# Halved weight loads, another product order and VectorE sums of x in a decoder layer on TensorE

## The chip, the cores and the metric

The kernel runs on one core of one Trainium2 chip. The metric is device time of one execution in microseconds (us), lower is better. Its engines are named as in the profile: PE is TensorE's matmuls and PEld its weight loads, DVE is VectorE, ACT is ScalarE, POOL is GpSimd and SP is SyncE, which here only issues DMAs. DMAs are issued by SP (hardware queue) and by POOL (software queue, which can also add what it loads to what lies in the buffer, an accumulating DMA).

## The reference

One decoder layer on a sequence of 1024 positions with 1024 channels, all in float32:

```python
h = rms_norm(x, g_mix)
z = h @ w_in + b_in                       # 1024 -> 7168 columns
va, ga, xb, gb, sa, sb = split(z)         # 1024, 1024, 1536, 1536, 1024, 1024
u = causal_conv31(va * sigmoid(ga));  u = silu(layer_norm(u));  y_a = u @ w_a_out
v = causal_conv4(xb);  v = rg_lru(v)      # gates: 16 heads of 96x96, then a linear recurrence
y_b = (v * gelu(gb)) @ w_b_out
m = sigmoid(sa) * y_a + sigmoid(sb) * y_b
x = x + m @ w_o
x = x + square(relu(rms_norm(x, g_mlp) @ w_1)) @ w_2
out = rms_norm(x, g_final)
```

A product in float32 is made of three matmuls in a faster format: each operand is split into a high part (the rounded value) and a low part (the rest), and high x high, high x low and low x high are added.

## The kernel before

Positions lie in the free dimension and channels on the partitions. The change touches the product with w_in, which is done in two parts.

**First part**, slots s = 3 to 27. Each slot makes one chunk of 128 columns of z (`chunk_mm`, L682): 48 matmuls of 128x128 by 128x512. The list `CH` gives their order: xb chunks (written XB + t, t = 0 to 11) and pairs of va and ga (VA + j, GA + j, j = 0 to 7). A slot's weight block is loaded two slots ahead by SP (`w_load`, win_raw) and split a slot ahead (`w_parts`): ScalarE writes a copy into the low part (L65) and the high part (L67), and POOL subtracts by an accumulating DMA (L66, win_l<-win_raw). That way of splitting is `split_dma`; the other, `split`, lets VectorE subtract (L414).

Behind a slot's chunk follows what hangs on the chunk before: `u_out` for a ga chunk (u, L541), or `xb_out` for an xb chunk, which writes xb and v on ScalarE (L426, L429) and queues the three further taps of v on VectorE (L438). `xb_parts`, one slot later, splits v: ScalarE writes vth (L446), VectorE the rest, vtl. `head_load` (SP, L463) gathers these into head tiles vh and vl. `head_mm(n, 0)` stands at the end of a head's slot and `head_mm(n, 1)` inside the next one (L486 to L488, 6 matmuls each); both write one and the same accumulator, which `head_gate` (ScalarE, L494) reads in between. Heads stand in slots 5 to 8, 10 to 13, 15 to 18 and 20 to 23. After each group of four, `scan_exp` and a slot later `scan_root` (ScalarE, with table loads, L510 to L518) and then `scan_tile` (VectorE, L527 to L530, 3 tiles a group) make the recurrence, whose result is stored to the scratch hd (L531).

VectorE fills the rest of its time with the taps of the width-31 convolution (`conv`, L571 to L603), 48 steps for each of 8 tiles of u; a finished tile is stored to yd (L597). `later` queues VectorE's work with the time at which it is ready, and `vector_work(end)` writes out the queue in order of those times, with convolution steps in between and then up to the planned time `end`. So the order on each engine is fixed when the kernel is built; at run time each engine works its list in order.

Most 128x1024 tiles (v, vth, vtl, g, a, u, y, xs and others) come from one pool of 37 buffers, and a new tile waits until the last reader of the tile before it in that buffer is done.

**Second part**, the columns gb, sa and sb, as 14 pairs of 128-column chunks. For each pair, a 2x2 block product (two columns by two halves of the channels, and two halves of the positions) is made with seven products instead of eight (Strassen's scheme in Winograd's form): 98 products of 12 matmuls (`z_mm`, L842). The list `zseq` holds their order as (pair, product). The sums of x that products 4 to 7 need are made at the end of the first part and the beginning of the second: `x_load`, `x_sum`, `x_parts`, placed by the table `XS` in slots 21 to 27. Before the change, `x_sum` lets ScalarE write a negated copy (L631) and POOL add the other block by an accumulating DMA from memory (L633).

A pair's weights are loaded by SP as two blocks, one for each column (`z_load`, L695, zw, 512 KB each, from a pool of four buffers), seven products ahead of the pair's first one (`z_load_to`). `z_sums` (VectorE) makes sums of weights four products ahead, `z_lhs` splits an operand three products ahead: by ScalarE (L65, L67) and an accumulating DMA (L66, zo<-zw or zo<-zs) for products 1, 2, 3, 4, 6, by ScalarE (L722) and VectorE (L414) for 5 and 7. `z_post` and `z_post2` copy an accumulator on (L878 to L889) or write an output: for gb, `z_out` takes a Gelu (ScalarE, L854), multiplies it with a half tile of the recurrence (hb, loaded from hd by `z_h`, L873, one product ahead) on VectorE (L857) and stores it to hgd (L858); for sa and sb it stores a sigmoid to the scratch gates (L865).

From the product behind the second part (yb, L91) on, nothing is changed.

Of the kernel before, what the change touches and what calls it, by code (L numbers as in the profile page):

```python
# [15 lines left out]
P = 128  # L16
# [14 lines left out]
def trunk_kernel(ctx: ExitStack, tc: tile.TileContext, x, xt_in, vecs, w_in, w_a_out, w_b_out,  # L31
# [12 lines left out]
    def T(name, dt=F32, shape=(P, S)):  # L44
        return tp.tile(list(shape), dt, tag="T", name=name)
# [17 lines left out]
    def split_dma(src, h, l):  # L63

        nc.scalar.activation(l, src, AF.Copy, scale=-1.0)  # L65
        nc.gpsimd.dma_start(l, src, accum_op=ALU.add)  # L66
        nc.scalar.activation(h, src, AF.Copy)  # L67
# [319 lines left out]
    def at(e, cost, ready=0.0):  # L387
        clk[e] = max(clk[e], ready) + cost
        return clk[e] + 0.1
# [225 lines left out]
    def x_load(c2):  # L615
        xq[c2] = q = {}
        for n in (11, 12):
            q[n] = T(f"xs{n}_{c2}")
            nc.sync.dma_start(q[n], x_blk(n, c2))

    def x_blk(n, c2):
        return xu[n % 10 - 1, 2 * (n // 10 - 1) + c2]

    def x_sum(c2, *ns):

        q = xq[c2]
        for n in ns:
            src, b = {11: (11, 12), 12: (12, 22), 22: (11, 22), 21: (22, 21)}[n]
            if n not in q:
                q[n] = T(f"xs{n}_{c2}")  # L630
            nc.scalar.activation(q[n], q[src], AF.Copy, scale=-1.0)  # L631
            at("A", 1.06)
            nc.gpsimd.dma_start(q[n], x_blk(b, c2), accum_op=ALU.add)  # L633

    def x_parts(c2, *ps):
        for p in ps:
            src = xq[c2][{6: 22, 7: 12, 5: 11, 4: 21}[p]]
            xbh[p][c2] = h = T(f"xs{p}h_{c2}", F32R)
            xbl[p][c2] = l = T(f"xs{p}l_{c2}", F32R)
            nc.scalar.activation(h, src, AF.Copy)  # L640
            later(at("A", 1.0), 1.2, nc.vector.tensor_tensor, l, src, h.bitcast(F32), ALU.subtract)
# [10 lines left out]
    def later(ready, cost, f, *a):  # L652

        todo.append((ready, len(todo), cost, f, a))
# [37 lines left out]
    def z_load(i):  # L692
        for m_ in range(2):
            zraw[i, m_] = raw = qp.tile([P, 8, P], F32, tag="p", name=f"zw{i}_{m_}", bufs=4)
            nc.sync.dma_start(raw, w_in[ZPAIRS[i] + m_])  # L695

    def z_blk(i, m_, kk):
        return zraw[i, m_][:, 4 * kk:4 * kk + 4, :]
# [34 lines left out]
    for i in range(2, NZ):  # L733
        zseq += [(i, 1), (i, 7), (i - 1, 3), (i, 6), (i, 2), (i - 1, 4), (i, 5)]
    zseq += [(NZ - 1, 3), (NZ - 1, 4)]
    def z_get(n, f):
# [8 lines left out]
    XS = {21: ((x_load, 0),), 22: ((x_sum, 0, 11, 12),), 23: ((x_sum, 0, 22), (x_load, 1)),  # L745
          24: ((x_sum, 0, 21), (x_sum, 1, 11, 12)), 25: ((x_sum, 1, 22),),
          26: ((x_parts, 0, 6, 7), (x_sum, 1, 21)), 27: ((x_parts, 0, 5, 4), (x_parts, 1, 6))}
# [3 lines left out]
    with tc.manual_schedule(engines=ENGINES):  # L751
        for s in range(3, NC1):
# [22 lines left out]
            if s == 4:  # L775
                xb_parts(0)
            elif CH[s - 2] >= XB:
                xb_parts(CH[s - 2] - XB)
# [24 lines left out]
            if s == NC1 - 3:  # L803
                z_load(0)
                z_load(1)
# [100 lines left out]
    loaded = 2  # L906

    def z_load_to(n):
        nonlocal loaded
        while loaded < min(len(zseq), n):  # L910
            if zseq[loaded][1] == 1:
                z_load(zseq[loaded][0])
            loaded += 1

    with tc.manual_schedule(engines=ENGINES):
# [40 lines left out]
        vector_work(clk["V"])  # L956
        for n in range(len(zseq) + 2):
            z_load_to(n + 7)
# [6 lines left out]
            if n + 1 < len(zseq):  # L965
                i, p = zseq[n + 1]
                if p in H_AT:
                    z_h(i, *H_AT[p])
# [61 lines left out]
    m = []  # L1030
# [678 lines left out]
```

## Time and profile before

| | |
|---|---|
| three runs | 1629.02, 1629.08, 1633.68 us, median 1629.08 |
| profiled execution | 1631.77 us, of which span 1630.0 |
| granted TensorE clock, mean | 0.993 |
| first part up to the first product of the second | 0 to 389 us of the span |
| second part | 389 to 686 us |
| the rest | 686 to 1630 us |
| PE busy, share of the span | 97% |
| DVE, ACT, POOL busy | 68%, 53%, 11% |
| DMA, hardware and software queue, share of 16 engines | 38.8% and 27.4% |

Engine rows of the profile give busy time, share and instructions. A group, a wait or a row of time names the engine, the line, the operation and out<-in by the program's tile names without their numbers. In a row of time the first number is the start in us, the second the length, and the bracket tells how long the engine had been idle before and what released it; "x3" means so many instructions in a row. A row of SPq or POOLq is that engine's DMA issue; where SP must wait to issue, its row is long. A matmul of 512 columns shows as 0.39 us but the next starts after 0.227, since matmuls overlap.

### The profile page before, as it was taken

Reading aid. Unit: us, or ns where it says so; the run is one execution under the profiler, and the core shown is the slowest. Engines: PE = TensorE matmul, PEld = TensorE weight load, DVE = VectorE, ACT = ScalarE, POOL = GpSimd, SP = SyncE. Lnnn points to the kernel's source line nnn. Section 1 sums busy time; section 2 is a strip of 40 time slices with the busy share of each in tenths; the row PEclk is TensorE's granted clock in tenths of the full one; section 3 lists DMA queues with packets and bytes.
Section 4 is the critical chain, followed back from the end, with each engine's and each line's share of the span. In section 5 each row is a group of like instructions: output and inputs, shape, how many; then the busy total and the mean of one; then the engine's idle time right before and its main releaser. Section 6 shows DMA issues by size and latency. Waiting matters only on the chain.

```text
span 1630.0 us, 18890 instructions
## 1 busy us (share of the span) xinstructions
PE 1577.1 (97%) x6910; PEld 1286.3 (79%) x6910; DVE 1115.9 (68%) x1488; ACT 858.2 (53%) x1136; POOL 176.1 (11%) x218
## 2 busy tenths in 40 slices
PE   8999999889988899899999999999999999999997
PEld 6878778767866787688888888788888888888886
DVE  6698989697777989537043136865555457888898
ACT  5538477457555665735252226654444366555552
POOL 0000000112111222101121100000000001111110
PEclk9999999999999999999999999999999999999999
DMA  9566887897787777965686442533333579888852
GB/s 368 151 172 176 217 210 199 207 266 171 206 218 193 183 186 184 298 214 143 161 208 179 117 137 83 194 123 111 103 116 118 175 233 220 224 218 211 217 129 104
DMA packets 101292, 299.14 MB, mean 184 GB/s; under 512 B 11424, under 2 KB 12960, under 8 KB 101200
## 3 DMA queue, kind: packets, MB, share of 16 engines
q1 hardware_dynamic: 70896, 208.04, 38.8%
q0 software_dynamic: 30160, 89.63, 27.4%
q8 instruction: 54, 0.88, 0.2%
q14 instruction: 38, 0.31, 0.1%
q10 hardware_dynamic: 144, 0.26, 0.0%
HBM read 146.11 MB, written 54.53 MB: 123 GB/s over the span
## 4 chain that ended last, share of the span: by engine, by line
PE 82%; issue 7%; DMA 5%; DVE 3%; ACT 1%; POOL 1%; SPq 0%; POOLq 0%; DVEq 0%; ACTq 0%
PE d L1492 14%; PE z L682 14%; PE yb L91 8%; PE ya L91 5%; PE o L1091 3%; PE e L1607 2%; DMA zo<-zw 2%; PE keep L1492 2%; PE o L91 2%; PE z L258 2%; DMA hd<-g 1%; PE rg L486 1%; PE rg L488 1%; PE rg L487 1%; DMA win_l<-win_raw 1%
## 5 line engine op out<-in xcount | busy, mean ns | idle before, releaser
L682 PE MATMUL z<-xh,win_h 128*128 128x512 f32 x400 | 125.4, 395 | 0.5 <-ACT win_h L67 0.5
L682 PE MATMUL z<-xl,win_h 128*128 128x512 f32 x400 | 124.4, 392 | 0.0
L1504 DVE TENSOR_TENSOR acc<-acc,d 128x1024 f32<-128x1024 f32 x72 | 87.9, 1220 | 33.3 <-PE d L1492 32.7
L682 PE MATMUL z<-xh,win_l 128*128 128x512 f32 x400 | 99.8, 396 | 3.4 <-DMA win_l<-win_raw 3.4
L682 PEld LDWEIGHTS z<-xh,win_l 128*128 128x128 f32 x400 | 76.2, 191 | 21.1 <-DMA win_l<-win_raw 3.9
L589 DVE SCALAR_TENSOR_TENSOR y<-u,vec,y 128x511 f32<-128x511 f32 (+14 forms) x120 | 88.5, 738 | 4.6 <-ACT y L571 4.6
L682 PEld LDWEIGHTS z<-xh,win_h 128*128 128x128 f32 x400 | 76.1, 191 | 17.9 <-ACT win_h L67 1.3
L682 PEld LDWEIGHTS z<-xl,win_h 128*128 128x128 f32 x400 | 76.2, 191 | 16.3
L494 ACT ACTIVATE g<-rg,vec 96x1024 f32<-96x1024 f32 x32 | 35.6, 1114 | 101.0 <-PE rg L488 51.6
L589 DVE SCALAR_TENSOR_TENSOR yt<-u,vec,yt 128x511 f32<-128x511 f32 (+6 forms) x112 | 82.7, 739 | 0.0
L589 DVE SCALAR_TENSOR_TENSOR y<-yt,csum,y 128x511 f32<-128x511 f32 (+6 forms) x112 | 82.7, 739 | 0.0
L438 DVE SCALAR_TENSOR_TENSOR v<-xb,vec,v 128x1023 f32<-128x1023 f32 (+2 forms) x36 | 46.2, 1283 | 20.9 <-ACT v L429 20.1
L1038 DVE TENSOR_TENSOR m<-yb,sb 128x1024 f32<-128x1024 f32 x8 | 9.8, 1225 | 71.9 <-PE yb L91 71.9
L1285 ACT ACTIVATE fa<-fa 128x512 f32<-128x512 f32 x16 | 10.1, 631 | 90.3 <-DVE fa L1263 90.3
L1225 ACT ACTIVATE o<-s 128x512 fp32r<-128x512 f32 x64 | 38.1, 622 | 29.5 <-DVE s L1217 26.1
L66 POOL DMA_DIRECT2D win_l<-win_raw x25 | 21.8, 872 | 291.7 <-ACT win_l L65 252.9
L66 POOL DMA_DIRECT2D zo<-zw x42 | 37.0, 889 | 96.9 <-ACT zo L65 71.6
L1139 DVE TENSOR_TENSOR o<-w_raw,o 128x512 fp32r<-128x512 f32 x40 | 27.5, 690 | 28.8 <-ACT o L1225 28.8
L1139 DVE TENSOR_TENSOR o<-s,o 128x512 fp32r<-128x512 f32 x64 | 42.6, 687 | 4.7 <-ACT o L1225 4.6
L1123 DVE TENSOR_TENSOR x<-xr,o 128x1024 f32<-128x1024 f32 x8 | 9.7, 1219 | 52.2 <-PE o L1091 37.7
L66 POOL DMA_DIRECT2D db_1l<-wr x7 | 6.1, 871 | 328.7 <-DMA wr<-in_w_dram 265.0
L1054 DVE TENSOR_TENSOR sa<-ya,sa 128x1024 f32<-128x1024 f32 x8 | 9.8, 1226 | 46.4 <-PE ya L91 46.4
(1582 smaller groups left out, 4638.2 us busy)
## 6 DMA issues: line engine op xcount, KB each, us to landing
fr<-fd SPq DMA_DIRECT2D x32, 512.0 KB, 5.8
wr<-in_w_dram SPq DMA_DIRECT2D x32, 512.0 KB, 6.3
w_raw<-in_w_dram SPq DMA_DIRECT2D x31, 512.0 KB, 4.4
zw<-in_w_in_dram SPq DMA_DIRECT2D x28, 512.0 KB, 4.3
win_raw<-in_w_in_dram SPq DMA_DIRECT2D x25, 512.0 KB, 6.8
win_l<-win_raw POOLq DMA_DIRECT2D x25, 512.0 KB, 6.1
zo<-zw POOLq DMA_DIRECT2D x42, 256.0 KB, 4.7
fd<-fa SPq DMA_DIRECT2D x16, 512.0 KB, 2.8
```

Source lines behind the costliest of these rows:

```text
L66: nc.gpsimd.dma_start(l, src, accum_op=ALU.add)
L91: nc.tensor.matmul(ps[:, HALVES[hf]], a, b[hf], start=i == 0, stop=i == len(todo) - 1)
L258: nc.tensor.matmul(z0[i][:, HALVES[hf]], w0[i][w][:, k, :], xpart(a, hf, k), start=k == 0 and which == "hh", stop=k == 7 and which == "hl" ...
L438: nc.vector.scalar_tensor_tensor(v[:, d:S], a[:, 0:S - d], cbw_c[:, w * 12 + t:w * 12 + t + 1], v[:, d:S], ALU.mult, ALU.add)
L494: nc.scalar.activation(a, gps.pop((n, gi))[:HD, :], AF.Sigmoid, bias=(ba_c, bx_c)[gi][:, n:n + 1])
L589: nc.vector.scalar_tensor_tensor(o[:, k:], a[:, 0:HS - k], c, o[:, k:], ALU.mult, add)
L682: nc.tensor.matmul(zps[s][:, HALVES[hf]], w[:, k, :], xw[k][part][hf], start=n == 0, stop=n == 23)
L1091: nc.tensor.matmul(ps[:, HALVES[hf]], tok(a, k, t), wo[k][b][:, HALVES[hf]], start=k == 0 and b == 0 and n == 0, stop=k == 7 and b == 1)
L1139: tt(l, src, h.bitcast(F32), ALU.subtract)
L1225: nc.scalar.activation(o[:, 0], src, AF.Copy)
L1492: nc.tensor.matmul(o, a, b, start=n == 0 and (p != 1 or g == 0), stop=n == len(todo) - 1, skip_group_check=p == 1 and g > 0)
L1504: tt(acc[p, q2], acc[p, q2], ps, ALU.add)
```

## The change

- The sums of x are made by VectorE. All four blocks of a half are loaded plainly by SP (8 loads in all, in slots 23 and 25, where before 4 were loaded in slots 21 and 23 and 8 added by POOL), and 8 subtractions on VectorE replace 8 ScalarE copies and 8 accumulating DMAs. Two of the eight splits of these sums go through `split_dma`.
- `xb_parts` follows `xb_out` in the same slot instead of in the next; the taps of v are written out ahead of it by `vector_work(0)`.
- A load of the second part's weights holds one half of the rows for both columns (two pieces of 2 KB for each partition) instead of all rows of one column (one piece of 4 KB). The first half is loaded seven products ahead of the pair's first one, the second five ahead (three for pair 2).
- In `zseq`, products 3 and 4 of the pair before change places, and the end has an order of its own.
- The loads of hb are issued three products ahead instead of one.

```diff
--- before.py
+++ after.py
@@ -613,32 +613,28 @@
     xq = {}
 
     def x_load(c2):
-        xq[c2] = q = {}
-        for n in (11, 12):
-            q[n] = T(f"xs{n}_{c2}")
-            nc.sync.dma_start(q[n], x_blk(n, c2))
-
-    def x_blk(n, c2):
-        return xu[n % 10 - 1, 2 * (n // 10 - 1) + c2]
-
-    def x_sum(c2, *ns):
-
+
+        xq[c2] = {n: T(f"xs{n}_{c2}") for n in (11, 12, 22, 21)}
+        for n, a in xq[c2].items():
+            nc.sync.dma_start(a, xu[n % 10 - 1, 2 * (n // 10 - 1) + c2])
+
+    def x_sum(c2):
         q = xq[c2]
-        for n in ns:
-            src, b = {11: (11, 12), 12: (12, 22), 22: (11, 22), 21: (22, 21)}[n]
-            if n not in q:
-                q[n] = T(f"xs{n}_{c2}")
-            nc.scalar.activation(q[n], q[src], AF.Copy, scale=-1.0)
-            at("A", 1.06)
-            nc.gpsimd.dma_start(q[n], x_blk(b, c2), accum_op=ALU.add)
+        for n, a, b in ((11, 12, 11), (12, 22, 12), (22, 22, 11), (21, 21, 22)):
+            later(0, 1.2, nc.vector.tensor_tensor, q[n], q[a], q[b], ALU.subtract)
 
     def x_parts(c2, *ps):
         for p in ps:
             src = xq[c2][{6: 22, 7: 12, 5: 11, 4: 21}[p]]
             xbh[p][c2] = h = T(f"xs{p}h_{c2}", F32R)
             xbl[p][c2] = l = T(f"xs{p}l_{c2}", F32R)
-            nc.scalar.activation(h, src, AF.Copy)
-            later(at("A", 1.0), 1.2, nc.vector.tensor_tensor, l, src, h.bitcast(F32), ALU.subtract)
+            if c2 == 0 and p < 6:
+                split_dma(src, h, l)
+                at("A", 2.0)
+            else:
+                nc.scalar.activation(h, src, AF.Copy)
+                later(at("A", 1.0), 1.2, nc.vector.tensor_tensor, l, src, h.bitcast(F32),
+                      ALU.subtract)
 
     CH = [XB, VA, GA, XB + 1, XB + 2]
     for js, g in (((1,), 1), ((2,), 2), ((3,), 3), ((4, 5, 6, 7), 4)):
@@ -689,13 +685,14 @@
     zraw, zs, zo, zb = {}, {}, {}, {}
     zn = [0]
 
-    def z_load(i):
-        for m_ in range(2):
-            zraw[i, m_] = raw = qp.tile([P, 8, P], F32, tag="p", name=f"zw{i}_{m_}", bufs=4)
-            nc.sync.dma_start(raw, w_in[ZPAIRS[i] + m_])
+    def z_load(i, kk):
+
+        zraw[i, kk] = raw = qp.tile([P, 2, 4, P], F32, tag="p", name=f"zw{i}_{kk}", bufs=4)
+        c = ZPAIRS[i]
+        nc.sync.dma_start(raw, w_in[c:c + 2, :, 4 * kk:4 * kk + 4, :].rearrange("m p k c -> p m k c"))
 
     def z_blk(i, m_, kk):
-        return zraw[i, m_][:, 4 * kk:4 * kk + 4, :]
+        return zraw[i, kk][:, m_]
 
     def z_sums(i, p):
 
@@ -731,8 +728,15 @@
     zseq = [(0, 1), (1, 1), (0, 2), (1, 2), (0, 6), (0, 7), (1, 7), (0, 5), (1, 6), (0, 3), (0, 4),
             (1, 5)]
     for i in range(2, NZ):
-        zseq += [(i, 1), (i, 7), (i - 1, 3), (i, 6), (i, 2), (i - 1, 4), (i, 5)]
-    zseq += [(NZ - 1, 3), (NZ - 1, 4)]
+        zseq += [(i, 1), (i, 7), (i - 1, 4), (i, 6), (i, 2), (i - 1, 3), (i, 5)]
+    zseq[-7:] = [(NZ - 1, p) for p in (1, 7, 6)] + [(NZ - 2, 4), (NZ - 1, 2), (NZ - 1, 5), (NZ - 2, 3)]
+    zseq += [(NZ - 1, 4), (NZ - 1, 3)]
+
+    ZL = {}
+    for i in range(2, NZ):
+        n = zseq.index((i, 1))
+        ZL[n - 7] = ((z_load, i, 0),)
+        ZL[n - (5 if i > 2 else 3)] = ((z_load, i, 1),)
     def z_get(n, f):
         return f(*zseq[n]) if 0 <= n < len(zseq) else None
 
@@ -742,9 +746,8 @@
     head_at = {s: n for n, s in enumerate(HS0)}
 
     EXP = {head_slot: g for g, head_slot in enumerate(HS0[4 * g + 3] + 1 for g in range(4))}
-    XS = {21: ((x_load, 0),), 22: ((x_sum, 0, 11, 12),), 23: ((x_sum, 0, 22), (x_load, 1)),
-          24: ((x_sum, 0, 21), (x_sum, 1, 11, 12)), 25: ((x_sum, 1, 22),),
-          26: ((x_parts, 0, 6, 7), (x_sum, 1, 21)), 27: ((x_parts, 0, 5, 4), (x_parts, 1, 6))}
+    XS = {23: ((x_load, 0),), 24: ((x_sum, 0),), 25: ((x_load, 1), (x_parts, 0, 6)),
+          26: ((x_sum, 1), (x_parts, 0, 7, 5)), 27: ((x_parts, 0, 4), (x_parts, 1, 6))}
     w_load(3)
     w_load(4)
     w_parts(3)
@@ -772,10 +775,9 @@
             elif c >= GA:
                 u_out(c - GA, zps[s - 2], zps[s - 1])
             w_parts(s + 1)
-            if s == 4:
-                xb_parts(0)
-            elif CH[s - 2] >= XB:
-                xb_parts(CH[s - 2] - XB)
+            if s == 3 or c >= XB:
+                vector_work(0)
+                xb_parts(0 if s == 3 else c - XB)
             if before is not None:
                 head_gate(before, 1, clk["P"] - 12 * MM)
             if nxt is not None:
@@ -801,8 +803,8 @@
             for f, *a in XS.get(s, ()):
                 f(*a)
             if s == NC1 - 3:
-                z_load(0)
-                z_load(1)
+                for i in range(4):
+                    z_load(i // 2, i % 2)
             vector_work(clk["P"] - 0.7)
             if nxt is not None:
                 head_load(nxt)
@@ -903,15 +905,6 @@
 
     ZX = {0: ((x_parts, 1, 7),), 7: ((later, 0, 4.8, scan_tile, 11),), 2: ((x_parts, 1, 5),), 4: ((x_parts, 1, 4),)}
     H_AT = {2: (0, 0), 5: (1, 1), 3: (0, 1), 4: (1, 0)}
-    loaded = 2
-
-    def z_load_to(n):
-        nonlocal loaded
-        while loaded < min(len(zseq), n):
-            if zseq[loaded][1] == 1:
-                z_load(zseq[loaded][0])
-            loaded += 1
-
     with tc.manual_schedule(engines=ENGINES):
 
         hg, hraw, wb0, wb0_ = [], {}, [], []
@@ -954,16 +947,18 @@
         z_get(2, z_lhs)
         u_out(7, zps[NC1 - 2], zps[NC1 - 1])
         vector_work(clk["V"])
+        z_h(0, 0, 0)
         for n in range(len(zseq) + 2):
-            z_load_to(n + 7)
+            for f, *a in ZL.get(n, ()):
+                f(*a)
             if n >= L:
                 for f, *a in ZX.get(n, ()):
                     f(*a)
             clk["A"], clk["V"] = max(clk["A"], clk["P"] + 0.5), max(clk["V"], clk["P"] - 2)
             z_get(n - 1, z_post)
             z_get(n - 2, z_post2)
-            if n + 1 < len(zseq):
-                i, p = zseq[n + 1]
+            if n + 3 < len(zseq):
+                i, p = zseq[n + 3]
                 if p in H_AT:
                     z_h(i, *H_AT[p])
             z_get(n, z_mm)
```

## The prediction

> **What bounds the kernel now.** I read the page's shares first, then the busy time by stage, then the waits of PE in the stages that the change touches, then the rows of time around the longest waits. The page:
>
> ```profile
> PE 1577.1 (97%) x6910; PEld 1286.3 (79%) x6910; DVE 1115.9 (68%) x1488; ACT 858.2 (53%) x1136; POOL 176.1 (11%) x218
> ```
>
> TensorE is the bound nearly throughout, and the change removes none of its matmuls. What it can win or lose is time in which PE waits, so I need where PE waits. Stretches of the span, PE to POOL in order, then granted clock, DMA share and GB/s:
>
> ```profile
> 50.00:280.00 230.00, 229.99 (x1008) 185.12 (x1007) 196.40 (x255) 141.95 (x147) 14.77 (x17) 1.00 0.75 192
> 280.00:389.00 109.00, 97.24 (x392) 76.43 (x392) 85.31 (x102) 65.33 (x70) 15.92 (x18) 0.92 0.89 225
> 389.00:430.00 41.00, 41.00 (x182) 33.95 (x182) 32.96 (x45) 27.21 (x45) 8.73 (x10) 1.00 0.66 173
> 430.00:540.00 110.00, 97.14 (x417) 76.95 (x416) 83.60 (x131) 57.85 (x99) 19.57 (x23) 1.00 0.75 194
> 540.00:620.00 80.00, 77.11 (x335) 62.23 (x334) 72.25 (x112) 49.49 (x86) 17.97 (x21) 1.00 0.77 191
> 620.00:686.00 66.00, 59.24 (x252) 47.17 (x251) 47.03 (x64) 44.37 (x71) 12.24 (x15) 0.99 0.89 246
> ```
>
> Two stretches show PE with hardly an idle moment and give its pace: 230.0/1008 = 0.228 us a matmul in the first part, 41.0/182 = 0.2253 in the second. At these paces the 392 matmuls of 280 to 389 need 89.4 of 109.0 us, so 19.6 us are lost there. In the second part (389 to 686) 430 to 620 holds 752 matmuls, 169.4 of 190 us, 20.6 lost; 620 to 686 holds 252, 56.8 of 66, 9.2 lost. The most that this change can win is thus about 49 us, unless it touches 686 onward, which it doesn't.
>
> **The end of the first part: removed stalls.** PE's waits, 280 to 390 (total, times, longest), and, in a second fence, rows of time around two of them:
>
> ```profile
> PE rg L486 <- ACT g L494: 4.2, 1, 4.2
> PE rg L486 <- DMA vh<-vth: 3.5, 1, 3.5
> PE z L682 <- DMA win_l<-win_raw: 3.4, 1, 3.4
> PE z L682 <- ACT win_h L67: 0.5, 1, 0.5
> ```
>
> ```profile
> 308.24 1.23 DVE L414 TENSOR_TENSOR vtl<-v,vth 128x1024 fp32r<-128x1024 f32 x1 [15.51 <-DMA hd<-g]
> ...
> 313.46 0.74 PE L486 MATMUL rg<-vh,rgh 96*96 96x512 f32 x1 [4.19 <-ACT g L494]
> ...
> 318.69 0.77 PE L682 MATMUL z<-xl,win_h 128*128 128x512 f32 x2
> ...
> 358.54 2.70 POOL L633 DMA_DIRECT2D xs<-xu  x3 [14.99 <-DVE yt L589]
> ...
> 361.23 0.92 POOL L66 DMA_DIRECT2D win_l<-win_raw  x1
> ...
> 372.80 5.52 PE L682 MATMUL z<-xh,win_l 128*128 128x512 f32 x16 [3.44 <-DMA win_l<-win_raw]
> ```
>
> The waits sum to 11.6 us; the rest of the 19.6 is the slow matmuls behind each long wait: 313.46 to 318.69 holds 12 in 5.23 us, 0.436 apiece, 2.5 us over the pace. Three times 2.5 and 11.6 are 19.1, so the account closes. The Trainium skill, TensorE: Matmul & The Clock Gate, Part 1, says that the clock halves after an idle window of some 3.4 us and returns after about as much busy time. The trace agrees in kind (4.2 us idle, then 0.436 us a matmul); by that page's 3.4 us at half pace a long stall's tail would be an estimated 1.7 us and my sum 0.8 us better.
>
> All three have one parent. The third is plain: the correction of a weight block was issued at 361.23 behind three accumulating loads of x on the same POOL queue and arrived 11.5 us later. The first begins where DVE waits 15.5 us for a store of a recurrence, whose buffer vtl takes over, while the plain loads of x occupy buffers and queues; the second is a landing in the same backlog. Transfers of 280 to 390, with KB and median us to landing:
>
> ```profile
> yd<-y SPq DMA_DIRECT2D x2, 512.0 KB, 11.3
> ...
> vh<-vth SPq DMA_DIRECT2D x1, 384.0 KB, 15.4
> ```
>
> After the change the first x loads come two slots later (slot 23) and the eight accumulating DMAs are gone, so the queue ahead of the block's correction is empty, vtl's buffer isn't taken by an x tile, and vh lands without that backlog. I take all four waits as gone: 19.6. Eight copies of 128x1024 (1.05 us by the row of 373.18 below) leave ScalarE. VectorE gets eight subtractions of 1.22 us (row of 308.24) and loses two low parts of x to an accumulating DMA on POOL (0.9 us of issue each, with POOL busy 15.9 of 109 us), 7.3 us net. It was busy for 85.3 of these 109 us, so some of its convolution taps slide into the second part. There it was busy 235.8 of 297 us, so that would fill 88% of a stretch shortened to 275. I price it at nothing; if that cover is gone, it costs up to 7.3.
>
> **Parts of v a slot sooner: an added wait.** ScalarE's high part of v now stands in the slot in which VectorE still adds three taps to v:
>
> ```profile
> 148.06 3.92 DVE L438 SCALAR_TENSOR_TENSOR v<-xb,vec,v 128x1023 f32<-128x1023 f32 x3 [0.99 <-ACT v L429]
> 149.82 1.04 ACT L446 ACTIVATE vth<-v 128x1024 fp32r<-128x1024 f32 x1
> 156.70 1.11 ACT L494 ACTIVATE g<-rg,vec 96x1024 f32<-96x1024 f32 x1
> 159.29 0.40 PE L486 MATMUL rg<-vh,rgh 96*96 96x512 f32 x1
> ```
>
> Now the copy at 149.82 is that of the chunk before. After the change ScalarE reaches there the copy of this chunk, and its v is ready at 151.98: 2.16 us of waiting, with the square roots, two table loads and the gate of 156.70 queued behind it. That gate then ends at 157.81 + 2.16 = 159.97, while the next head's first matmul, which writes the same accumulator, was due at 159.29: 0.7 us. This chain with the roots stands in slots 10, 15 and 20: 2.1 us in all. In the other slots the gate ends early enough. Bounds: nothing, if ScalarE had room elsewhere, and three times 2.2.
>
> **A new stall at the last slot.** Four x loads, then four loads of the second part's weights, now stand on SP ahead of the store of the last convolution but one. Its buffer is wanted by the next tile of taps. On VectorE a recurrence is queued behind that, and ScalarE's u waits for the recurrence's buffer; the last weight block's copies stand behind u.
>
> ```profile
> 363.06 0.69 DVE L580 TENSOR_TENSOR yt<-u 128x512 f32<-128x512 f32 x1
> ...
> 364.24 1.22 DVE L527 SCALAR_TENSOR_TENSOR g<-a,g 128x1024 f32<-128x1024 f32 x1
> ...
> 366.88 2.29 DVE L530 TENSOR_TENSOR_SCAN g<-a,g 128x1024 f32<-128x1024 f32 x1
> ...
> 369.92 1.28 ACT L541 ACT_TABLE_LOAD   x1
> ...
> 371.22 1.11 ACT L541 ACTIVATE u<-z,vec 128x1024 f32<-128x1024 f32 x1
> ...
> 373.18 1.05 ACT L67 ACTIVATE win_h<-win_raw 128x1024 fp32r<-128x1024 f32 x1
> ...
> 378.16 0.62 PE L682 MATMUL z<-xh,win_h 128*128 128x512 f32 x2
> ```
>
> Now this tile's taps end at 361.9; less the lost time ahead of it (19.6 without the last wait's 3.9 and the tail's 2.5) they would end at 348.7, and as one slot's filler goes elsewhere I take 346.5. For the store I take 8 us, less than the 11.3 of its row because the accumulating loads are gone: landed 354.5. From 363.06 to the recurrence's end at 369.17 the row takes 6.1 us, so 360.6; then 1.28, 1.11 and two copies of 1.05 make 365.1. The last slot started at 378.2 and without the 19.6 but with one 0.7 would start at 359.3. PE waits 5.8 us, with a slow tail of 2.5: 8.3. Bounds: nothing (landing 6 us sooner), and 12 (landing in the row's 11.3). First part: 19.6 − 2.1 − 8.3 = 9.2 us won.
>
> **Second part: what makes PE wait there.** PE's waits from 380 to 690 (two of sixteen lines), the landing of the hb loads there, and one pair's rows:
>
> ```profile
> PE z6e L842 <- DVE zo L414: 2.4, 1, 2.4
> ...
> PE z13f L842 <- DMA zo<-zw: 2.2, 1, 2.2
> ```
>
> ```profile
> hb<-hd SPq DMA_DIRECT2D x24, 256.0 KB, 4.9
> ```
>
> ```profile
> 489.45 6.03 SPq L858 DMA_DIRECT2D hgd<-hb  x2
> ...
> 495.20 0.61 ACT L65 ACTIVATE zo<-zw 128x512 fp32r<-128x512 f32 x1
> ...
> 495.57 5.50 SPq L695 DMA_DIRECT2D zw<-in_w_in_dram  x2
> ...
> 496.11 0.88 POOL L66 DMA_DIRECT2D zo<-zw  x1 [2.30 <-ACT zo L65]
> ...
> 500.63 0.73 PE L842 MATMUL z5a<-xh,zo 128*128 128x512 f32 x2 [1.47 <-DMA zo<-zw]
> ...
> 506.11 0.69 DVE L857 TENSOR_TENSOR hb<-hb,ze 128x512 f32<-128x512 f32 x1 [4.50 <-DMA hb<-hd]
> ...
> 507.46 0.72 PE L842 MATMUL z5e<-xs5h,zo 128*128 128x512 f32 x2 [1.08 <-DVE zo L414]
> ```
>
> SP stands still for 6.0 and again 5.5 us, waiting to load weights into a buffer that is still being read. The loads of the recurrence results (hb) queue behind it. So DVE stands 4.5 us at 506.11, and a low part behind it holds PE at 507.46; ScalarE, held by the same chain, copies a weight at 495.20 instead of soon after 490, and the correction lands at 500.6, 1.5 us late. In 540 to 620, where hb loads end, only 4.5 us are lost; in 430 to 540 it is 16.0.
>
> The change undoes this in two ways. The load by row halves serves both columns, so the first half is needed early and the second late; in the new order each buffer's last reader lies several products before the load that takes it, so SP needn't stand. And hb is asked for three products ahead, one product being 12 × 0.2253 = 2.7 us, against a landing of 4.9. What is late next is the correction for (i,2): from its slot's start 0.5 of lead, a copy out of PSUM, a gate and the weight's copy (each taken at 0.6, by the row of 495.20) lead to POOL at +2.4 with what POOL needs to start, landing takes 4.5 (496.11 to 500.63), so +6.9 against 3 × 2.7 = 8.1. Margin 1.2 us. So I take the 20.6 of 430 to 620 as gone. In 620 to 686 the gates' reloads compete with the same corrections and the change leaves them; I keep 7.5 of the 9.2, since only ScalarE's copy ahead of z13e is moved away by the new last order. Second part: 20.6 + 1.7 = 22.3. Bounds: 5 (only the hb waits go) and 26. A load by halves has rows of 2 KB instead of 4 KB; I price that at nothing, for at 0.75 the DMA share leaves room; without it, the margin of 1.2 would go.
>
> **Sum.** 9.2 + 22.3 = 31.5 us. The profiled execution took 1631.8 (span 1630.0), giving 1600.3; the runs' median of 1629.1 gives 1597.6. I take 1599.
>
> **Rivals.** (B) *Corrections keep PE waiting in the second part.* From 540 to 620 there is hardly an hb and 4.5 us are lost all the same. If 2 KB rows or a busier VectorE eat the 1.2 us, a wait of about 0.8 at each of two products in eleven pairs, 17, comes back, and the part wins only 5: 1631.8 − 9.2 − 5, about 1617. (C) *No stall at the last slot*, the store landing by 349: 8.3 more, 40 won, 1591. (D) *The change does not move what it says*: ScalarE reaches u and the weight copies no sooner, and VectorE sets the second part; gains of 5 and new waits cancel: 1629. (E) *Slower*: VectorE reaches v's taps late in most slots, because the steps of a recurrence (4.9 us, from 364.24 to 369.17) stand in front. ScalarE's wait of 2.2 becomes 7.1, exceeds the 1.5 us of room at 157.81 by 5.6, and each such slot costs 5.6 + 2.5 = 8.1. Four slots eat the whole gain; at six of the twelve it is 49 − 31, about 1649. For it: VectorE is 85% busy from 50 to 280. Against: at 148.06 it was VectorE that waited for v, 0.99 us.
>
> **Chances.** Forecast 0.50 (1590 to 1611), B 0.18, C 0.12, D 0.05, E 0.15. The range reaches from C's 1588 over B to 1624 and leaves out E and part of D. Differences of 0.3%, 4.9 us, are what the runs can tell from none: faster 0.80, within it 0.05, slower 0.15.
>
> **What would show it.** Right: no accumulating x loads and no PE wait over 3 us from 295 to 375 except one at the last slot, with the clock row dipping once; the second part about 275 us long; no SP rows of 5 us for zw; waits for DVE zo gone. Wrong: PE waits for gates in nearly every early slot (E), corrections of zo<-zw still listed for most pairs (B), DVE near 100% in the second part.

## The result and the profile after

The changed kernel takes 1617.19 us (median of 4 runs, 1616.07 to 1620.73) against 1630.32 us before (4 runs): a ratio of 0.992 with a 95% interval of 0.9897 to 0.9943, 13.1 us faster. The forecast was 1599, about 31 us faster; 1617 lies inside the stated range and meets the sum of rival B, but not its parts: B gave 9.2 us to the first part and 5 to the second, and 3.4 and 11.0 were measured (below), so that the sums agree is luck. The profiled execution took 1616.91 us (span 1615.1), 14.9 less than the one before.

The page of the changed kernel, its first and clock rows:

```profile
PE 1569.0 (97%) x6910; PEld 1283.4 (79%) x6910; DVE 1125.1 (70%) x1494; ACT 850.9 (53%) x1130; POOL 170.6 (11%) x212
...
PEclk9999999998999999999999999999999999999999
```

Stretches of the changed kernel (PE, PEld, DVE, ACT, POOL busy, clock, DMA share, GB/s), cut where its second part begins and ends:

```profile
50.00:280.00 230.00, 228.64 (x1002) 183.76 (x1001) 206.78 (x270) 143.84 (x148) 14.77 (x17) 1.00 0.76 193
280.00:386.00 106.00, 94.23 (x402) 75.57 (x401) 82.80 (x94) 59.10 (x64) 10.50 (x12) 0.94 0.80 218
...
430.00:540.00 110.00, 102.33 (x442) 81.88 (x441) 95.73 (x148) 66.04 (x114) 22.69 (x26) 1.00 0.85 211
540.00:620.00 80.00, 79.91 (x353) 65.76 (x352) 72.85 (x113) 47.50 (x85) 18.17 (x21) 1.00 0.73 185
620.00:672.00 52.00, 45.70 (x197) 36.18 (x196) 33.26 (x42) 33.37 (x52) 8.89 (x11) 1.00 0.92 266
```

And the first matmul of the second part and of what follows it:

```profile
385.66 0.39 PE L844 MATMUL z0a<-xh,zo 128*128 128x512 f32 x1
...
671.67 0.62 PE L91 MATMUL yb<-hgh,wb0h 128*128 128x512 f32 x2
```

The second part began at 389.04 and ended at 686.06 before; now it runs from 385.66 to 671.67. So 3.4 us were won up to its start (forecast 9.2) and 11.0 in it, 297.0 to 286.0 (forecast 22.3). From 540 to 620 PE is full, 353 matmuls in 80 us; from 430 to 540 there are 442 where 488 would go at 0.2253 us each, 10.4 us lost (16.0 before). PE's waits from 45 to 690, the longest of the list:

```profile
PE z L678 <- ACT win_h L67: 11.1, 1, 11.1
PE rg L486 <- ACT g L494: 2.0, 3, 0.7
PE z12a L844 <- DMA zo<-zw: 2.0, 1, 2.0
PE z5a L844 <- DMA zo<-zw: 1.6, 1, 1.6
PE z13f L844 <- DVE zc L414: 1.6, 1, 1.6
PE z3a L844 <- DMA zo<-zw: 1.5, 1, 1.5
PE z6a L844 <- DMA zo<-zw: 1.3, 1, 1.3
```

The three waits of the old end of the first part are gone, and so are those for VectorE's low parts (DVE zo). In their place stand one of 11.1 us at the last slot and, in seven of the fourteen pairs (3 to 7, 12 and 13), a wait at the first accumulator (z3a, z5a, z6a), which is product 2's correction. The three waits for gates are those of slots 11, 16 and 21, 0.7 each as forecast. Of the signs named for being right, all but the length of the second part are there: POOL adds no x, PE waits over 3 us only at the last slot, the clock row dips once, and no row of SP for zw in the second part is longer than 0.5 us. Of those for being wrong, B's is there, in half of the pairs.

The chain at the last slot, rows of time of the changed kernel:

```profile
341.01 6.19 SPq L619 DMA_DIRECT2D xs<-xu  x4
...
347.29 2.66 SPq L692 DMA_DIRECT2D zw<-in_w_in_dram  x4
...
350.71 0.34 SPq L597 DMA_DIRECT2D yd<-y  x1
...
361.67 0.69 DVE L580 TENSOR_TENSOR yt<-u 128x512 f32<-128x512 f32 x1 [9.73 <-DMA yd<-y]
...
365.50 2.29 DVE L530 TENSOR_TENSOR_SCAN g<-a,g 128x1024 f32<-128x1024 f32 x1
...
367.87 1.28 ACT L541 ACT_TABLE_LOAD   x1 [5.49 <-DVE g L530]
...
371.12 1.05 ACT L67 ACTIVATE win_h<-win_raw 128x1024 fp32r<-128x1024 f32 x1
...
372.22 1.22 PE L678 MATMUL z<-xh,win_h 128*128 128x512 f32 x2 [11.10 <-ACT win_h L67]
```

Each link is the one forecast, in the forecast order: the store of the convolution tile behind the x and zw loads, VectorE waiting 9.7 us for it, the recurrence, ScalarE's u, the weight block, PE. Its size is another: the store was issued at 350.7, not 346.5, and landed 10.9 us later, not 8. The 12 matmuls from 372.22 to 377.47 take 0.437 us apiece, 2.5 us over the pace.

And one pair of the second part:

```profile
486.05 0.32 SPq L860 DMA_DIRECT2D hgd<-hb  x1
...
486.25 0.87 POOL L66 DMA_DIRECT2D zo<-zw  x1 [2.61 <-ACT zo L65]
...
486.46 0.39 SPq L692 DMA_DIRECT2D zw<-in_w_in_dram  x1
...
486.94 0.93 SPq L875 DMA_DIRECT2D hb<-hd  x2
...
487.15 0.87 POOL L66 DMA_DIRECT2D zo<-zs  x1
...
494.31 0.73 PE L844 MATMUL z5a<-xh,zo 128*128 128x512 f32 x2 [1.64 <-DMA zo<-zw]
```

POOL issues product 2's correction at 486.25, about 2.6 us into its slot, as forecast (+2.4). But 0.2 us later SP issues 512 KB of weights and then two hb loads, and POOL another correction: 1.5 MB within 1.2 us. The correction needs 8.0 us instead of the 4.5 in the sum, and PE waits 1.6. By the trace this is so in each of pairs 3 to 6: the 512 KB follow product 2's correction by 0.2 to 0.4 us, it lands 7.4 to 8.1 us after its issue, and PE waits 0.9 to 1.6, 5.3 in all.

### The profile page after: what moved, and what is told of

Same layout as the page of the kernel before. It is cut to its first block, busy times and chain, and to the rows that moved or that the text cites. A ratio compares the mean times of both kernels' runs of the same rounds, so it can differ in the third digit from the quotient of the medians.

```text
span 1615.1 us, 18841 instructions
## 1 busy us (share of the span) xinstructions
PE 1569.0 (97%) x6910; PEld 1283.4 (79%) x6910; DVE 1125.1 (70%) x1494; ACT 850.9 (53%) x1130; POOL 170.6 (11%) x212
## 4 chain that ended last, share of the span: by engine, by line
PE 79%; issue 7%; DMA 5%; ACT 4%; DVE 3%; POOL 1%; SPq 0%; POOLq 0%; ACTq 0%; DVEq 0%
PE d L1487 14%; PE z L678 11%; PE yb L91 8%; PE ya L91 5%; DMA zo<-zw 3%; PE o L1086 3%; PE e L1602 2%; PE keep L1487 2%; PE o L91 2%; PE z L258 2%; POOL zo L66 1%; PE rg L486 1%; PE rg L488 1%; PE rg L487 1%; PE o L1110 1%
## 5 line engine op out<-in xcount | busy, mean ns | idle before, releaser
L678 PE MATMUL z<-xh,win_h 128*128 128x512 f32 x400 | 124.9, 394 | 11.1 <-ACT win_h L67 11.1
```

The costliest lines, as they stand in the source:

```text
L678: nc.tensor.matmul(zps[s][:, HALVES[hf]], w[:, k, :], xw[k][part][hf], start=n == 0, stop=n == 23)
```

## Experiments

Each run's time is compared with the kernel before on the same chip. The first product and the length of the second part are from its profile, that is from one execution. What follows the second part takes 943.1 to 944.2 us in every profile, so the executions of one kernel differ in the two parts of the table, and they do differ: p_hb's whole times go from 1616.0 to 1625.8 us, and p_v, which leaves the second part as it was, has 292.9 there against 297.0. A difference of up to some 4 us between two such lengths proves nothing alone. One correction to the description ahead of the prediction, on which two expectations rest: counted exactly, the kernel before loads a pair's weights six products ahead, not seven (`z_load_to(n + 7)` takes the products up to n + 6); the changed kernel's first half is seven ahead.

| kernel | ratio to before (95%) | first product, us | second part, us |
|---|---|---|---|
| before | 1 | 389.0 | 297.0 |
| changed | 0.992 (0.9897 to 0.9943) | 385.7 | 286.0 |
| e_x_old | 0.9933 (0.9917 to 0.995) | 389.9 | 284.2 |
| e_columns | 0.9903 (0.9887 to 0.9919) | 385.7 | 283.2 |
| e_order | 0.9886 (0.9869 to 0.9903) | 384.3 | 279.7 |
| e_hb_one | 0.9933 (0.9918 to 0.9948) | 386.8 | 289.3 |
| e_store_first | 0.9887 (0.987 to 0.9904) | 379.6 | 285.6 |
| e_half_later | 0.9868 (0.9851 to 0.9885) | 385.4 | 278.0 |
| e_hb_only | 0.9854 (0.9834 to 0.9875) | 384.6 | 275.8 |
| e_both | 0.9838 (0.9822 to 0.9855) | 372.9 | 284.8 |
| p_hb | 0.9959 (0.9942 to 0.9975) | 391.3 | 288.1 |
| p_v | 0.9988 (0.9977 to 1.0) | 388.8 | 292.9 |
| p_load7 | 0.9956 (0.9938 to 0.9974) | 389.7 | 286.4 |
| p_hb_load7 | 0.9899 (0.9873 to 0.9924) | 389.3 | 276.7 |
| e_hb_load6 | 0.9915 (0.9883 to 0.9947) | 385.9 | 285.8 |
| e_best_a | 0.9833 (0.9818 to 0.9848) | 378.5 | 275.6 |
| e_best_b | 0.9825 (0.9811 to 0.984) | 373.5 | 279.8 |

### One part undone at a time

**e_x_old**: the changed kernel with x_load, x_sum, x_parts and the table XS of before.

```diff
...
-            later(0, 1.2, nc.vector.tensor_tensor, q[n], q[a], q[b], ALU.subtract)
...
+            nc.scalar.activation(q[n], q[src], AF.Copy, scale=-1.0)
...
+            nc.gpsimd.dma_start(q[n], x_blk(b, c2), accum_op=ALU.add)
...
```

> The changed kernel with the sums of x made as before (ScalarE copies and accumulating loads, first loads in slot 21). Theory (two places of loss: the convolution store that waits behind x and zw loads before the last slot, and in the second part a bunch of transfers behind each second half load): the wait at the last slot (11.1 us) shrinks or goes, the waits of 3 to 4 us of the old end of the first part return; first product of the second part between 380 and 391 (now 385.7), second part 283 to 289 us (now 286.0), time 1611 to 1623. Rival (VectorE's 7.3 us of added subtractions set the second part): second part 279 or less.

Measured: 1619.38 us, first product 389.9, second part 284.2. The old waits are back (win_raw 5.9, vh 3.9) and the one at the last slot is down to 2.2. So VectorE's sums of x are worth 4.2 us in the first part; the 1.8 us that the second part is shorter without them are too few to tell from none, and VectorE's added 7.3 us do not set the second part.

**e_columns**: the changed kernel with whole columns (z_load(i, m) loads one column, in pieces of 4 KB). Not the pieces alone change: the second load comes seven products ahead instead of five, and SP then waits for its buffer.

```diff
...
-        ZL[n - 7] = ((z_load, i, 0),)
-        ZL[n - (5 if i > 2 else 3)] = ((z_load, i, 1),)
+        ZL[n - 7] = ((z_load, i, 0), (z_load, i, 1))
```

> The changed kernel with the second part's weights loaded as whole columns (4 KB pieces, both seven products ahead), all else as changed. Theory: SP stands again at a load whose buffer is still read, 5 us and more a pair, with hb behind it; second part 290 to 298 us (now 286.0), time 1621 to 1629. Rival (pieces of 2 KB are what makes corrections land late): second part 275 to 283, time under 1614.

Measured: 1614.84 us, second part 283.2, 2.8 less. The theory fell: SP does stand again (rows of zw of 5.5 to 6.3 us from 430 on), and PE waits no more than before the edit. The rival's bounds were missed narrowly, and 2.8 us are too few to tell from none.

**e_order**: the changed kernel with the old list of products.

```diff
-        zseq += [(i, 1), (i, 7), (i - 1, 4), (i, 6), (i, 2), (i - 1, 3), (i, 5)]
-    zseq[-7:] = [(NZ - 1, p) for p in (1, 7, 6)] + [(NZ - 2, 4), (NZ - 1, 2), (NZ - 1, 5), (NZ - 2, 3)]
-    zseq += [(NZ - 1, 4), (NZ - 1, 3)]
+        zseq += [(i, 1), (i, 7), (i - 1, 3), (i, 6), (i, 2), (i - 1, 4), (i, 5)]
+    zseq += [(NZ - 1, 3), (NZ - 1, 4)]
```

> The changed kernel with the product order of before (3 before 4, old end), all else as changed. Theory: the buffer for a second half is then read up to the correction of product 4 three products later, so the half lands late and its sums hold PE: second part 290 to 300 us (now 286.0). Rival (the order matters only at the end): within 2 us of 286.0.

Measured: 1610.35 us, second part 279.7. Both expectations missed: the new order costs 6.3 us. The trace says how: with the old order the load of the second half follows product 2's correction by 0.6 to 0.8 us in pairs 2 to 6, the correction lands after 4.8 to 6.0 us, and PE waits for it in none of these pairs, against 5.3 us in pairs 3 to 6 of the changed kernel. In both kernels the load is the next on SP behind a store of hgd, which waits for VectorE's product; in pairs 3 to 6 that store comes 0.1 to 0.2 us ahead of the correction with the new order and 0.2 to 0.3 behind it with the old.

**e_hb_one**: the changed kernel with hb one product ahead.

```diff
...
-            if n + 3 < len(zseq):
-                i, p = zseq[n + 3]
+            if n + 1 < len(zseq):
+                i, p = zseq[n + 1]
```

> The changed kernel with hb loaded one product ahead as before, all else as changed. Theory: the bunch behind the second half load loses two of its five transfers, corrections of product 2 land 1.5 to 2.5 us sooner and their waits (about 1.5 us a pair in pairs 3 to 7) go, but VectorE waits for hb: second part 281 to 290. Rival (the earlier hb brought the gain): 292 or more.

Measured: 1618.74 us, second part 289.3, 3.3 more. Within the theory's band, though its reason held in part only: z5a waits 0.8 instead of 1.6, but z3a 2.4 instead of 1.5. The 3.3 us themselves are within what two such lengths differ by.

### The two causes, tried directly

**e_store_first**: the four first weight loads behind the convolution's store.

```diff
-            if s == NC1 - 3:
-                for i in range(4):
-                    z_load(i // 2, i % 2)
             vector_work(clk["P"] - 0.7)
+            if s == NC1 - 3:
+                for i in range(4):
+                    z_load(i // 2, i % 2)
```

> The changed kernel with the first four weight loads of the second part issued behind the store of the convolution tile instead of ahead of it. Theory (the wait of 11.1 us at the last slot hangs on this store, which lands 10.9 us after its issue behind those loads): the store lands 4 to 6 us after its issue, the wait falls to about 5 us, the first product of the second part comes at 378 to 381 (now 385.7), time 1609 to 1613 against the changed kernel's 1617. Rival (VectorE's order, with the added subtractions, holds the last slot): first product within 2 us of 385.7.

Measured: 1610.73 us, first product 379.6, second part unchanged at 285.6. The store landed 4.3 us after its issue. PE's wait in this kernel, and VectorE's for the store (from the tile yd):

```profile
PE z L678 <- ACT win_h L67: 4.8, 1, 4.8
```

```profile
  DVE yt L580: 3.1, 1
```

The wait falls from 11.1 to 4.8 and VectorE's from 9.7 to 3.1. That settles the last slot: the order of four loads and one store on SP was worth 6 us.

**e_half_later**: the second half's load three products ahead for every pair, behind the hb loads on SP instead of ahead of them.

```diff
-        ZL[n - (5 if i > 2 else 3)] = ((z_load, i, 1),)
+        ZL[n - 3] = ((z_load, i, 1),)
```

> The changed kernel with the second half of a pair's weights loaded three products ahead instead of five. Theory (that load is released together with the correction of product 2, overtakes it, and hb loads follow in the same microsecond): corrections of product 2 land in 5 to 6.5 us instead of 8.0, their waits in pairs 3 to 7 go, second part 278 to 282 us (now 286.0). Rival (the load's lead is needed): new waits on sums of weights, second part 288 or more.

Measured: 1608.06 us, second part 278.0. The same pair, rows of SP and POOL, and PE's waits at two of the places:

```profile
481.90 0.32 SPq L860 DMA_DIRECT2D hgd<-hb  x1
482.31 0.86 SPq L875 DMA_DIRECT2D hb<-hd  x2
483.23 0.47 SPq L692 DMA_DIRECT2D zw<-in_w_in_dram  x1
```

```profile
482.11 0.87 POOL L66 DMA_DIRECT2D zo<-zw  x1 [2.61 <-ACT zo L65]
```

```profile
PE z3a L844 <- DMA zo<-zw: 0.6, 1, 0.6
...
PE z5a L844 <- DMA zo<-zw: 0.3, 1, 0.3
```

The 512 KB now follow the correction by 1.1 us instead of 0.2; z5a waits 0.3 instead of 1.6, z3a 0.6 instead of 1.5. In pairs 3 to 6 the correction now lands after 5.1 to 7.1 us. Moving one load by two products, and behind the hb loads, won 8 of the 11 us that the forecast had too many.

### What of the second part's edits pays

**e_hb_only**: e_columns and e_order together, so that of these edits the earlier hb (and, as it turned out, one product more of lead for the weights) is left.

> The changed kernel with whole columns loaded seven products ahead and the product order of before, so that of the second part's edits only the earlier hb is left. Theory (in the second part before, hb behind a standing SP is what costs most, halves and order little or less than nothing): second part 278 to 288 us. Rival (only halves and order together free SP): 292 or more, as SP stands 5 us for zw again.

Measured: 1605.62 us, second part 275.8, below the theory's band. Median landing of the corrections from 430 to 620, first in the changed kernel, then here:

```profile
zo<-zw POOLq DMA_DIRECT2D x29, 256.0 KB, 5.3
...
zo<-zs POOLq DMA_DIRECT2D x18, 256.0 KB, 5.5
```

```profile
zo<-zw POOLq DMA_DIRECT2D x30, 256.0 KB, 3.6
zo<-zs POOLq DMA_DIRECT2D x20, 256.0 KB, 4.1
```

And yet SP stands longer here than it ever did. Rows of POOL, then of SP (a row of two issues holds the wait between them):

```profile
481.36 1.77 POOL L66 DMA_DIRECT2D zo<-zw  x2 [2.99 <-ACT zo L65]
```

```profile
484.74 0.33 SPq L690 DMA_DIRECT2D zw<-in_w_in_dram  x1
...
529.34 15.16 SPq L690 DMA_DIRECT2D zw<-in_w_in_dram  x2
...
549.02 14.75 SPq L690 DMA_DIRECT2D zw<-in_w_in_dram  x2
```

Product 2's correction for the same pair was issued by POOL at 481.36, and the load of the second column 3.4 us behind it, at 484.74. SP's wait ahead of that load ends, by the trace's semaphores, with the landing of this very correction at 484.60, so the load cannot get ahead of it. So it is in all of pairs 2 to 12: the correction lands 3.2 to 3.3 us after its issue, the load follows the landing by 0.1 to 0.2 us, and PE waits for product 2 in none of them.

**p_hb, p_load7, p_hb_load7** take the kernel before and move hb two products ahead, the weights one product ahead, and both; **e_hb_load6** is e_hb_only with the weights six ahead again.

The weights, in p_load7 and p_hb_load7:

```diff
-            z_load_to(n + 7)
+            z_load_to(n + 8)
```

hb, in p_hb and p_hb_load7:

```diff
+        z_h(0, 0, 0)
...
-            if n + 1 < len(zseq):
-                i, p = zseq[n + 1]
+            if n + 3 < len(zseq):
+                i, p = zseq[n + 3]
```

> The kernel before with one edit: hb loaded three products ahead instead of one. Theory (hb behind a standing SP is the whole loss that the change wins back in the second part): second part 274 to 280 us (before 297.0, changed 286.0), time 1607 to 1612. Rival (hb ahead is worth this only with the first part's new order): 285 or more.

> The kernel before with one edit: whole columns loaded one product sooner. Theory: hb still queues one product ahead behind the standing load, so little is won: second part 291 to 299 us. Rival (the load's lead is the whole gain): 282 or less.

> The kernel before with two edits: hb three products ahead, and whole columns loaded one product sooner (counted exactly, before loads them six products ahead and the changed kernel's first half seven). Theory (both leads together make the second part run; first part plays no role): second part 274 to 279 us (before 297.0, with the earlier hb alone 288.1). Rival (the first part's new order is needed for it): 284 or more.

> The changed kernel with old product order and whole columns loaded six products ahead, hb three ahead; against the run with seven products (second part 275.8). Theory (one product of lead is worth the difference of 12 us between that run and the kernel before with the earlier hb): second part 284 to 290 us. Rival (it was the first part): 274 to 278.

Measured, second part: p_hb 288.1 (1622.85 us), p_load7 286.4 (1621.35), p_hb_load7 276.7 (1613.12), e_hb_load6 285.8 (1616.78). The theory of p_hb, that hb alone is the loss, fell, and so did both expectations of p_load7; the other two hold. p_hb's length lies in its rival's band, but the rival's reason, the first part, fell with p_hb_load7. In these profiles each lead alone is worth 9 to 11 us and both 20.3; by the medians of the whole times it is 5.0, 6.3 and 14.5, as the profiled execution of the kernel before (1631.8) was slower than its medians beside these runs (1627.7 and 1627.8). The first part plays no role (276.7 with the old, 275.8 with the new). Each lead removes waits of its own. Those of PE for VectorE's low parts (DVE zo) sum to 6.7 us before, 5.0 with the weights' lead alone and none with hb's; those for corrections of zo<-zw to 13.2 before, 10.6 with hb's lead alone and 5.8 with the weights'. The longest of each kind that is left, first in p_load7, then in p_hb (there at a pair's first product):

```profile
PE z4e L842 <- DVE zo L414: 1.7, 1, 1.7
```

```profile
PE z5a L842 <- DMA zo<-zw: 2.8, 1, 2.8
```

With six products of lead and the earlier hb, the waits are again at product 2 or 1 of a pair; in e_hb_load6:

```profile
PE z13a L840 <- DMA zo<-zw: 3.9, 2, 2.7
PE z5a L840 <- DMA zo<-zw: 2.6, 1, 2.6
```

Together with e_columns and e_order this gives, in us of the second part (weights seven products ahead, the second of the halves five):

| hb three products ahead | old order | new order |
|---|---|---|
| whole columns | 275.8 | 283.2 |
| halves of rows | 279.7 | 286.0 |

The order costs 6.3 and 7.4 us, clear of what such lengths differ by. The halves cost 2.8 and 4.0, which is at that limit, and with them go the second load's lead and what it waits for: in the old order it follows product 2's correction by 0.6 to 0.8 us as a half and by 3.3 to 3.4 as a column. What pieces of 2 KB cost by themselves was not tried.

**p_v** is the kernel before with the parts of v in v's own slot.

```diff
-            if s == 4:
-                xb_parts(0)
-            elif CH[s - 2] >= XB:
-                xb_parts(CH[s - 2] - XB)
+            if s == 3 or c >= XB:
+                vector_work(0)
+                xb_parts(0 if s == 3 else c - XB)
```

> The kernel before with one edit: parts of v in the slot of v itself. Theory (ScalarE's wait for the taps costs PE about 1 us in each of slots 11, 16 and 21, nothing elsewhere): first product of the second part 1 to 4 us later than 389.0 in the profile, three waits for gates of 0.7. Rival (splitting v sooner frees buffers and so removes waits of the old end of the first part): 3 us or more sooner.

Measured: 1626.22 us against 1627.83, ratio 0.9988 (0.9977 to 1.0). The three gates wait as expected (2.0 in all), but the first product comes at 388.8, not later: the wait of 4.2 us at 313 is gone, and the one for win_raw grew from 3.4 to 6.1. Neither expectation holds; alone this edit moves the time by about nothing.

### Versions that beat both

**e_both** is e_order, the store first, and the last weight block's two copies emitted on ScalarE ahead of its wait; **e_best_a** is e_hb_only with the store first; **e_best_b** is e_best_a with these copies ahead as well.

```diff
-            w_parts(s + 1)
+            if s != NC1 - 2:
+                w_parts(s + 1)
...
+            if s == NC1 - 3:
+                w_parts(NC1 - 1)
             vector_work(clk["P"] - 0.7)
```

> The changed kernel with the old product order, the four weight loads behind the convolution store, and the last weight block's copies on ScalarE ahead of that wait. Theory: no long wait at the last slot, first product of the second part at 372 to 377, second part 278 to 281 us, time 1597 to 1603. Rival (another wait takes the place at the last slot, or the second part's start waits for the operands instead): first product at 380 or later, time 1606 or more.

> The changed kernel with whole columns and the old product order (of the second part's edits only the earlier hb) and the first four weight loads behind the convolution store. Theory (the parts add): first product at 378 to 381, second part 275 to 279, time 1598 to 1601. Rival (the later weight loads cost at the start of the second part what they win): 1603 or more.

> As e_best_a, and the last weight block's copies on ScalarE ahead of the wait for the store. Theory: first product at 372 to 375, but its operands arrive late and the second part is 278 to 283; time 1595 to 1601. Rival (the sum of x's splits and the first operands bind ScalarE, so nothing is won): within 1.5 us of e_best_a.

Measured: e_both 1603.12 us, first product 372.9 as expected, but a second part of 284.8 where 278 to 281 were expected, as its first operands come late (z0a waits 2.6). e_best_a 1599.18 us; e_best_b 1598.50 us, 0.9825 of before. The parts add in e_best_a: 378.5 and 275.6. In e_best_b 4.2 of the 5.0 us won ahead of the second part are lost again in it (279.8), as the theory had it, and for the whole time the rival is right too: within 1 us of e_best_a. PE's waits in e_best_b, from 45 to 690:

```profile
PE z13e L843 <- ACT zc L890: 2.4, 1, 2.4
PE rg L486 <- ACT g L494: 2.0, 3, 0.7
PE z L678 <- ACT u L541: 1.7, 1, 1.7
PE z11a L843 <- DMA zo<-zw: 1.4, 1, 1.4
```

## Why the prediction was wrong in size

**The old waits at the end of the first part (19.6 us).** Right. None of the three is left, and e_x_old brings two of them back.

**The gates of slots 11, 16 and 21 (2.1 us).** Right: three waits of 0.7, 2.0 in all; each of these slots takes 0.9 us more than before (slot 11 14.65 against 13.73).

**The last slot (8.3 us).** Mechanism right, size wrong. Two terms failed: the tile's end (346.5 taken, 350.7 found) and the store's landing (8 taken, 10.9 found, though the row of before quoted there, the median of two stores, said 11.3; this store itself took 9.5). Together they are 7.1 us. The last slot also began at 361.1 instead of 359.3, for the sum counted one gate there and three came. So the wait was 5.3 us longer, 11.1 instead of 5.8, with its tail 13.6; with the gates' 0.7 over the 2.1 that takes the first part from 9.2 to 3.2, and 3.4 were measured. I had lowered both numbers from their rows for reasons that no row showed; why the tile ended so late was not tried.

**The second part (22.3 us).** The two leads are worth nearly that in the profiles: 20.3 in p_hb_load7, 21.3 in e_hb_only, where 275.8 us are left against the 274.7 that the sum implied (14.5 for p_hb_load7 by the medians). What failed is the pricing of halves and order at nothing. They take back 10.3 us together (the table of four), 6.3 to 7.4 for the order and the rest for what goes with the halves. The step that broke is "margin 1.2 us" for product 2: its issue was right, its landing of 4.5 us was read from a pair in which SP issued nothing for 4.6 us behind the correction, and the change puts a 512 KB load and two hb loads there, with which it lands after 7.4 to 8.1 us in pairs 3 to 6. This is rival B by its place; its cause was neither of those named for it, but what stands behind the correction on SP. The runs show it by the distance between the two in these pairs: 0.2 to 0.4 us in the changed kernel with 5.3 us of waits, 0.6 to 0.8 in e_order and 3.3 to 3.4 in e_hb_only with none. What 2 KB pieces cost by themselves stays open.

**SP standing still.** I took SP's standing as the harm, 6.0 and 5.5 us at loads of zw. The first of these was misread: the row at 489.45 is two stores of hgd, and between them SP waits for the product that the second one stores, a row of VectorE in the kernel before:

```profile
494.45 0.68 DVE L857 TENSOR_TENSOR hb<-hb,zu 128x512 f32<-128x512 f32 x1
```

The store follows at 495.16, and the first weight load stood behind it on SP without a wait of its own (495.57). Only the second, of 5.5 us, waits for a buffer of weights. Nor was standing the harm: in e_hb_only SP stands up to 14 us between the two loads of a pair and PE waits least. What hurt was what stood behind with too little lead, and a load that waits for a correction to land also keeps its bytes away from it. I also counted the old lead of the weights as seven products where it was six, and so missed that the change lengthens it.

**VectorE.** The cover held: 95.7 of 110 us busy from 430 to 540 and, by e_x_old, no more than 1.8 us lost in the second part. Rival E did not occur; up to 310 us p_v shows no wait beyond the three.

**The clock.** Behind the 11.1 us the matmuls ran 2.5 us over the pace, as in the sum, behind the 4.8 us of e_store_first 2.1. The 2.5 was no constant, though: it is 1.6 in e_hb_only behind 10.4 us and 3.0 in e_columns behind 10.6, and behind the third old wait it was 1.7. By the Trainium skill, TensorE: Matmul & The Clock Gate, Part 1, it would be an estimated 1.7; these runs show 1.6 to 3.1.

## What to carry to other kernels

A landing time belongs to what else is issued around it: before you reuse one, list what the changed order puts on every queue within a microsecond or two of that issue, and price the landing from a row with such neighbours. An in-order DMA queue that stands at a wait is not a loss by itself; ask what is behind it and how much lead that has. And when several edits come together, measure them apart: here two leads won 15 to 20 us, and two other edits gave back up to 10.

## What the hardware showed that I had not expected

A correction of 256 KB (accumulating, on POOL) landed 3.2 to 3.3 us after its issue in pairs 2 to 12 of e_hb_only, with nothing on SP behind it for 3.3 us, and 7.4 to 8.1 us in pairs 3 to 6 of the changed kernel, with a 512 KB load on SP 0.2 to 0.4 us behind it and loads of hb behind that. A later transfer on the other queue can get through first: in pair 5 that load landed at 494.02, the correction at 494.26. A delay of the load by about 1 us, with the hb loads moved ahead of it, brought PE's wait for the correction there from 1.6 to 0.3 us.
